# Strided attention on one core: eighteen pair buffers instead of sixteen quad buffers, one eviction per group

## The chip, the cores and the metric

The kernel runs on one core of a Trainium2 chip. The metric is the device time of one execution in microseconds; the median over three runs is given with its lowest and highest. A profile of one execution shows what each engine and the DMA queue did. Its span runs from the first to the last instruction and is a little shorter than the device time.

## What is computed

Q, K and V are float32 arrays of shape (8, 12, 1024, 64): 96 heads, 1024 positions, 64 channels. With stride 64, each query attends to the 16 positions 0, 64, 128, ... of its head:

```python
attend_positions = np.arange(0, seq, stride)
k = K[:, :, attend_positions, :]
v = V[:, :, attend_positions, :]
scores = np.einsum('bhqd,bhkd->bhqk', q, k) / np.sqrt(dim)
weights = np.exp(scores - np.max(scores, axis=-1, keepdims=True))
weights = weights / (np.sum(weights, axis=-1, keepdims=True) + 1e-10)
result[:, :, i, :] = np.einsum('bhqk,bhkd->bhqd', weights, v)[:, :, 0, :]
```

All of Q is read (25.2 MB), the output has the same size, and of K and V only one row in 64 is read. There are 1,024 times 96 rows of 16 scores.

## The kernel before

**Groups.** The 96 heads are cut into 24 groups of four heads (`NG`, `HG`). A group is 1 MB of Q and 1 MB of output, 128 partitions of 2048 float32 each. A buffer `qn[g % BUFS]` first receives a group of Q and later holds the same group's output, from which it is stored. There are 16 such buffers, in four tiles (`quads`) of four groups, so that a store of four groups reads one contiguous run of each partition.

**One group's way through the engines.** GpSimd casts Q to bfloat16 (`cast`, line 306; the first three are shared with ScalarE). VectorE transposes it in 32 x 32 blocks (`transpose`, line 317). TensorE makes the scores against the group's 16 keys per head (`score_products`). VectorE takes each row's maximum and subtracts it (`largest`). ScalarE takes the exponential (`raise_`, line 347). VectorE sums and takes reciprocals (`sums`). GpSimd multiplies (`weights`, line 359). TensorE transposes the weights (`turn_products`), ScalarE spreads them into a block layout with two instructions (`spread`, line 378), TensorE multiplies with the values (`output_products`, eight products into four PSUM banks, `o_ps`), and ScalarE evicts the result into the group's buffer (`evict`, line 406). The eviction is in two halves of 1024 columns: half 0 after the first four products, half 1 after the other four. There is one `o_ps`, so the products of group g+1 wait for the evictions of group g, half by half.

**The order of the work.** `Program` records every operation in one list, with what it reads and writes, and derives from it the semaphore waits; each engine executes its operations in the order of the list. The list is written by the loop over `i` at line 507, which calls the steps of `ORDER` (line 506) for group `i` minus the number behind the step's name. So in step i, ScalarE spreads group i-3, evicts group i-4 and takes the exponential of group i-1.

**TensorE's loop and the gates.** TensorE's instructions are a hardware loop of 14 passes with two turns each (`pe_stream`, line 512), so 28 turns for 24 groups: turn i makes the scores of group i, turns the weights of group i-2 and multiplies out group i-3, each after waiting on a counting semaphore called a gate: `turned`, `weighted`, `free0`, `free1`. The first and last turns work on dummy groups; dummy operations (`free`, a no-op on ScalarE; memsets of `edge`; counts of three) raise the gates for them. An instruction that raises a gate raises no other semaphore, so whoever waits for such an instruction waits for the next one on the same engine that doesn't raise a gate (line 103).

**Loads and stores.** All go through SP and one DMA queue. First the strided rows of K, then group 0, the rows of V, and groups 1 to 15. Each transfer is issued with a hand-built instruction, `_copy` (line 25). `queue` (line 468) puts the stores into SP's order: `STORES` gives runs of 4, 2, 2, 4, 4, 4, 2 and 2 groups. After the third store SP issues the eight late loads (groups 16 to 23), each of which waits for the store that empties its buffer. The last store is issued outside the list (line 537), after ScalarE's last eviction; GpSimd meanwhile waits for the older stores and clears the semaphores.

Of the kernel before, what the change touches and what calls it, by code (L numbers as in the profile page):

```python
# [168 lines left out]
def kernel(  # L169
# [14 lines left out]
    P = 128  # L184
# [6 lines left out]
    BUFS = 16  # L191
    RUN = 4
# [6 lines left out]
    quads = [sb.tile([P, RUN, 32 * D], FP32, name=f"quad{i}") for i in range(BUFS // RUN)]  # L199
    qn = [quads[i // RUN][:, i % RUN] for i in range(BUFS)]  # L200
# [7 lines left out]
    k_t = sb.tile([P, NG + 4, 2, 4 * NK], BF16, name="k_t")  # L208
    v_all = sb.tile([P, NG + 4, 4, D], BF16, name="v_all")
# [101 lines left out]
    def transpose(g):  # L311
        k_in = {0: "0", 1: "1"}.get(g)
        words = qt[g % 2].bitcast(I32)
        if g >= NG:
            op("DVE", lambda: nc.vector.memset(edge[:, g - NG : g - NG + 1], 0.0), gate="turned", times=1 if g == NG else 3)
# [42 lines left out]
    def weights(g):  # L358
        op("POOL", lambda: nc.gpsimd.tensor_tensor(  # L359
            out=wt[g % 2], in0=ex[g % 2],  # L360
            in1=rec[g % 2].unsqueeze(2).to_broadcast([P, 32, NK]), op=ALU.mult,
        ), reads=[f"ex{g % 2}", f"rec{g % 2}"] + [k for k in apart if k[0] == "v"], writes=[f"wt{g % 2}"], gate="weighted", times=1 if g < NG - 1 else 3)
# [33 lines left out]
    def outputs(g, n):  # L396
        op("PE", None, reads=[f"wb{g % 2}0", f"wb{g % 2}1"] + [
               f"v{g % 2}{a}{b}{int(g >= 4)}" if 0 <= g < NG else "none" for a in range(2) for b in range(2)
           ], writes=[f"o{n}"], gates=[(f"free{n}", g + 1)] if g >= 0 else [], looped=True)

    def evict(g, n):
        to = qn[g % BUFS].rearrange("p (b c x d) -> p c b (x d)", b=2, c=4, d=D)
        half = slice(2 * n, 2 * n + 2)
        plain = g >= NG - 1 - 2 * n
        ready = [f"wb{(g + 1) % 2}0", f"wb{(g + 1) % 2}1"] * (n == 0)
        op("ACT", lambda: nc.scalar.copy(  # L406
            to[:, half], o_ps[:, half].rearrange("p c (b x) -> p c b x", b=2)
        ), reads=[f"o{n}"] + ready, writes=[f"qn{g % BUFS}{n}"],
           gate=None if plain else f"free{n}", last=g == NG - 1 and n == 1)

        if plain:
            free([f"qn{g % BUFS}{n}"], n)

    def free(reads, n):
        op("ACT", lambda: nc.scalar.nop(), reads=reads, gate=f"free{n}")  # L415

    def send(g, n):
# [3 lines left out]
            _ap_with(qn[g % BUFS], [quads[0].ap[0], [1, 1], [1, 32 * n * D]]),  # L421
# [6 lines left out]
    def idle(i):  # L428
        scores(i)
        turn(i - 2)  # L430
        for n in range(2):
            outputs(i - 3, n)
# [29 lines left out]
    turns = (NG + 4) // TURN  # L462

    STORES = [4, 2, 2, 4, 4, 4, 2, 2]
    assert sum(STORES) == NG
    STORED = {sum(STORES[: i + 1]) - 1: n for i, n in enumerate(STORES)}

    def queue(g):
        if g not in STORED or g == NG - 1:
            return  # L470
        store(g - STORED[g] + 1, STORED[g])
        if g == NG - BUFS - 1:
            for n in range(BUFS, NG):
                load(n)

    def at(i, stage, lag):
# [5 lines left out]
        elif stage == "scores" and 0 <= g < NG + 4:  # L482
# [3 lines left out]
        elif stage == "turn" and 0 <= g < NG + 2:  # L486
            turn(g)
        elif stage in ("outA", "outB") and -1 <= g < NG + 1:
            outputs(g, int(stage == "outB"))
        elif stage == "spread" and 0 <= g < NG:  # L490
            spread(g)
        elif stage in ("evA", "evB") and g == -1:
            n = int(stage == "evB")
            free(["wb00", "wb01"], n)
        elif stage in ("evA", "evB") and 0 <= g < NG:
            evict(g, int(stage == "evB"))
# [9 lines left out]
    ORDER = "transpose0 cast-1 turn3 spread3 sums2 values2 weights2 outA4 largest1 evA4 outB4 evB4 scores0 raise_1 queue4".split()  # L506
# [5 lines left out]
    def pe_stream(sems, gates):  # L512
# [3 lines left out]
        for n in range(2):  # L516
            pe.sem_inc(gates[f"free{n}"], 3)
        with pe.Fori(0, turns) as turn_:
            for j in range(TURN):
# [5 lines left out]
                for n in range(2):  # L525
# [11 lines left out]
    end = send(NG - STORES[-1], STORES[-1])  # L537
# [34 lines left out]
```

## Time and profile before

| | |
|---|---|
| Median of 3 runs | 128.75 us (128.72 to 128.87) |
| The profiled execution: its own time | 128.75 us |
| The profiled execution: span | 126.9 us |
| TensorE matmuls, busy | 66.9 us (53%) |
| VectorE, busy | 88.0 us (69%) |
| ScalarE, busy | 97.6 us (77%) |
| GpSimd, busy | 75.9 us (60%) |
| Moved by DMA | 51.16 MB, 403 GB/s over the span |
| Granted TensorE clock, mean | 0.86 |

Times in the profile are in microseconds from the start of the span. PE is TensorE, PEld its weight loads, DVE VectorE, ACT ScalarE, POOL GpSimd, SP SyncE; SPq is SP's own instruction queue. A line of the slices gives, for 40 equal slices of the span, the busy share in tenths (9 means 90% or more). A row of a DMA queue gives packets, MB, and the time that its packets took as a share of 16 engines' span. A row of the stretches gives from:to and length, then for each engine the busy time with the number of instructions, then the granted TensorE clock, the DMA engines' busy share and the GB/s. A row of the timeline gives start, duration, engine, line and operation, with written tile, read tile and count, and in brackets the idle time before it and what ended it. A row of the DMA view gives the size and the time from issue to landing. A row of the waits gives who waited for whom: microseconds in total, times, longest. A row for one line's instructions gives durations in ns: least, median, greatest.

### The profile page before, as it was taken

Reading aid. Unit: us, or ns where it says so; the run is one execution under the profiler, and the core shown is the slowest. Engines: PE = TensorE matmul, PEld = TensorE weight load, DVE = VectorE, ACT = ScalarE, POOL = GpSimd, SP = SyncE. Lnnn points to the kernel's source line nnn. Section 1 sums busy time; section 2 is a strip of 40 time slices with the busy share of each in tenths; the row PEclk is TensorE's granted clock in tenths of the full one; section 3 lists DMA queues with packets and bytes.
Section 4 is the critical chain, followed back from the end, with each engine's and each line's share of the span. In section 5 each row is a group of like instructions: output and inputs, shape, how many; then the busy total and the mean of one; then the engine's idle time right before and its main releaser. Section 6 shows DMA issues by size and latency. Waiting matters only on the chain.

```text
span 126.9 us, 2253 instructions
## 1 busy us (share of the span) xinstructions
PE 66.9 (53%) x784; PEld 49.3 (39%) x784; DVE 88.0 (69%) x131; ACT 97.6 (77%) x133; POOL 75.9 (60%) x67
## 2 busy tenths in 40 slices
PE   0005796677836456586530394557856478771000
PEld 0004585455734334364320373335624356550000
DVE  3585979999899999999980779999999773000000
ACT  4147758999999999999993199999999999991000
POOL 5637698999999777797403996777793332000000
PEclk9999999965799999959996579998599955999755
DMA  0999999899998989989999999999999999999980
GB/s 23 418 320 465 392 454 465 372 475 392 444 475 361 465 361 485 454 351 423 418 470 434 413 454 392 465 434 403 454 385 457 423 423 444 392 398 434 429 382 21
DMA packets 5413, 51.16 MB, mean 403 GB/s; under 512 B 3616, under 2 KB 3616, under 8 KB 3616
## 3 DMA queue, kind: packets, MB, share of 16 engines
q1 hardware_dynamic: 5408, 51.12, 95.8%
q14 instruction: 5, 0.04, 0.1%
HBM read 25.95 MB, written 25.17 MB: 403 GB/s over the span
## 4 chain that ended last, share of the span: by engine, by line
DMA 30%; ACT 22%; POOL 21%; DVE 6%; issue 6%; PE 4%; SPq 1%; ACTq 0%; POOLq 0%
DMA out_dram<-quad 14%; ACT quad L406 13%; POOL qb L306 12%; DMA quad<-in_Q_dram 10%; ACT wb_all L378 7%; POOL wt_all L359 6%; DMA v_raw<-in_V_dram 6%; DVE qt L317 3%; ACT ex L347 3%; POOL v_all L288 2%; PE o L386 2%; DVE total L352 1%; SPq L34 1%; PE tp L366 1%; DVE top L339 1%
## 5 line engine op out<-in xcount | busy, mean ns | idle before, releaser
L406 ACT COPY quad<-o 128x1024 f32<-128x1024 f32 x48 | 46.3, 1015 | 2.2
L306 POOL CAST qb<-quad 128x2048 bf16<-128x2048 f32 x21 | 39.7, 1889 | 6.9 <-DMA quad<-in_Q_dram 6.8
L386 PE MATMUL o<-v_all,wb_all 128*128 x224 | 39.0, 317 | 2.4 <-ACTq L415 0.7
L359 POOL TENSOR_TENSOR wt_all<-ex,rec 128x512 bf16<-128x512 f32 x24 | 25.4, 1057 | 18.5 <-DVE rec L355 18.1
L378 ACT ACTIVATE wb_all<-tp,sel 128x512 bf16<-128x512 bf16 x48 | 30.4, 690 | 5.6 <-PE tp L366 5.4
L317 DVE STREAM_TRANSPOSE qt<-qb 128x1024 int32<-128x1024 int32 x24 | 29.7, 1237 | 5.2 <-POOL qb L306 5.0
L325 PE MATMUL sc<-k_t,qt 128*128 x448 | 23.3, 210 | 16.2 <-DVE qt L317 11.8
L325 PEld LDWEIGHTS sc<-k_t,qt 128*128 128x128 bf16 x448 | 20.4, 109 | 21.8 <-issue 19.6
L366 PE MATMUL tp<-identity,wt_all 128*128 128x128 bf16 x112 | 13.0, 249 | 29.8 <-POOL wt_all L359 29.8
L386 PEld LDWEIGHTS o<-v_all,wb_all 128*128 128x128 bf16 x224 | 22.9, 114 | 11.2 <-ACT quad L406 4.9
L352 DVE TENSOR_REDUCE total<-ex 128x32 f32<-128x512 f32 x24 | 16.3, 677 | 7.0 <-ACT ex L347 7.0
L366 PEld LDWEIGHTS tp<-identity,wt_all 128*128 128x128 bf16 x112 | 7.6, 109 | 32.6 <-POOL wt_all L359 32.6
L342 DVE TENSOR_TENSOR low<-sc,top 128x512 f32<-128x512 f32 x24 | 16.6, 691 | 0.8
L347 ACT ACTIVATE ex<-low 128x512 f32<-128x512 f32 x24 | 15.4, 641 | 2.1 <-DVE low L342 2.0
L339 DVE TENSOR_REDUCE top<-sc 128x32 f32<-128x512 f32 x24 | 15.2, 632 | 1.3 <-PE sc L325 1.3
L355 DVE RECIPROCAL rec<-total 128x32 f32<-128x32 f32 x24 | 8.5, 353 | 0.8
L288 POOL CAST v_all<-v_raw 32x128 bf16<-32x128 f32 (+1 forms) x12 | 5.2, 430 | 1.1 <-DMA v_raw<-in_V_dram 0.4
L302 POOL CAST qb<-quad 128x1024 bf16<-128x1024 f32 x3 | 3.1, 1037 | 4.3 <-DMA quad<-in_Q_dram 4.2
L300 ACT CAST qb<-quad 128x1024 bf16<-128x1024 f32 x3 | 3.1, 1045 | 2.4 <-DMA quad<-in_Q_dram 2.4
L264 ACT CAST k_half<-k_raw 128x768 bf16<-128x768 f32 x1 | 0.8, 831 | 3.2 <-DMA k_raw<-in_K_dram 3.2
L260 POOL MEMSET v_all<- 128x3584 f32 x1 | 3.1, 3085 | 0.0
L288 ACT CAST v_all<-v_raw 32x640 bf16<-32x640 f32 x4 | 2.9, 722 | 0.0
(15 smaller groups left out, 10.3 us busy)
## 6 DMA issues: line engine op xcount, KB each, us to landing
quad<-in_Q_dram SPq DMA_DIRECT2D x24, 1024.0 KB, 17.3
out_dram<-quad SPq DMA_DIRECT2D x4, 4096.0 KB, 18.3
out_dram<-quad SPq DMA_DIRECT2D x4, 2048.0 KB, 12.8
k_raw<-in_K_dram SPq DMA_DIRECT2D x1, 384.0 KB, 4.9
v_raw<-in_V_dram SPq DMA_DIRECT2D x1, 384.0 KB, 7.0
```

Of the source, the lines that this page charges most:

```text
L306: op("POOL", lambda: nc.gpsimd.tensor_copy(out=b, in_=q), reads=[f"qn{g % BUFS}{h}" for h in range(2)] + apart, writes=[f"qb{g % 2}{h}" fo ...
L317: op("DVE", lambda: nc.vector.transpose(_ap_with(words, [words.ap[0], [1, 2], [D, 16], [2, 32]]), qb[g % 2].bitcast(I32),), reads=[f"qb{g ...
L325: r = nc.tensor.matmul(sc_ps[g % 2][:, 64 * i : 64 * i + 64], lhsT=_ap_with(qt[g % 2], [qt[g % 2].ap[0], [2, P]], extra_offset=2 * P * i + f),
L339: op("DVE", lambda: nc.vector.tensor_reduce(out=m, in_=s, op=ALU.max, axis=mybir.AxisListType.X,), reads=[f"sc{g % 2}"], writes=[f"top{g % ...
L342: op("DVE", lambda: nc.vector.tensor_tensor(out=low, in0=s, in1=m.unsqueeze(2).to_broadcast([P, 32, NK]), op=ALU.subtract,), reads=[f"sc{g ...
L347: op("ACT", lambda: nc.scalar.activation(out=ex[g % 2], in_=low, func=AF.Exp, bias=0.0, scale=scale,), reads=["low"], writes=[f"ex{g % 2}"])
L352: op("DVE", lambda: nc.vector.tensor_reduce(out=total[g % 2], in_=ex[g % 2], op=ALU.add, axis=mybir.AxisListType.X,), reads=[f"ex{g % 2}"] ...
L359: op("POOL", lambda: nc.gpsimd.tensor_tensor(out=wt[g % 2], in0=ex[g % 2], in1=rec[g % 2].unsqueeze(2).to_broadcast([P, 32, NK]), op=ALU.mult,
L366: r = nc.tensor.transpose(tp_ps[g % 2][:, 2 * c : 2 * c + 2].rearrange("p a b -> p (a b)"), wt[g % 2][:, 8 * c : 8 * c + 8].rearrange("p t ...
L378: op("ACT", lambda a=a: nc.scalar.activation(out=wb[g % 2][:, :, 64 * a : 64 * a + 64], in_=tp_ps[g % 2], func=AF.Copy, scale=sel[:, a : a ...
L386: r = nc.tensor.matmul(_ap_with(o_ps, [o_ps.ap[0], [128, 2], [256, 2], [1, D]], extra_offset=512 * c + D * u,), lhsT=wb[g % 2][:, 2 * c + ...
L406: op("ACT", lambda: nc.scalar.copy(to[:, half], o_ps[:, half].rearrange("p c (b x) -> p c b x", b=2)), reads=[f"o{n}"] + ready, writes=[f" ...
```

## The change

- The buffers become 18, in nine tiles (`pairs`) of two groups. Eighteen loads stand in front; six are late.
- Stores are of two groups, in order, the last two groups in a store each. After the store of groups 2-3 SP gets the loads of 18 and 19, after 4-5 those of 20 and 21, after 6-7 those of 22 and 23. A load waits for the landing of the store that empties its buffer, as before. The step `queue` moves from lag 4 to lag 5.
- A group's output is evicted by one ScalarE instruction of 2048 columns, and one gate, `free`, stands for all of `o_ps`. Eight products follow one wait.
- TensorE's loop has 13 passes of two turns, 26 turns; the output products of the last group are recorded behind the loop with ordinary waits. The dummies for the last turns go, as do the no-ops on ScalarE; the second half of group 0's spread raises the gate for the dummy group -1. `k_t` and `v_all` have fewer slots.
- The rows of K and V are loaded with the library's `dma_start` instead of the hand-built copy.

```diff
-    BUFS = 16
-    RUN = 4
+    BUFS = 18
+    RUN = 2
...
-        op("SP", lambda: _copy(
-            nc, tile_, _ap_with(src, kv_src),
-        ), writes=[name], lane=lane)
+        op("SP", lambda: nc.sync.dma_start(tile_, _ap_with(src, kv_src)),
+           writes=[name], lane=lane)
...
-            ), reads=[f"tp{g % 2}", "sel"], writes=[f"wb{g % 2}{a}"])
-
-    def output_products(g, k, n):
-        for c in range(2 * n, 2 * n + 2):
+            ), reads=[f"tp{g % 2}", "sel"], writes=[f"wb{g % 2}{a}"], gate="free" if a and not g else None)
+
+    def output_products(g, k):
+        for c in range(4):
...
+    def outputs(g):
+        last = g == NG - 1
+        op("PE", (lambda: output_products(g, g + 3)) if last else None, reads=[f"wb{g % 2}0", f"wb{g % 2}1"] + [
                f"v{g % 2}{a}{b}{int(g >= 4)}" if 0 <= g < NG else "none" for a in range(2) for b in range(2)
-           ], writes=[f"o{n}"], gates=[(f"free{n}", g + 1)] if g >= 0 else [], looped=True)
+           ], writes=["o"], gates=[("free", g + 1)] if g >= 0 and not last else [], looped=not last)
...
         op("ACT", lambda: nc.scalar.copy(
-            to[:, half], o_ps[:, half].rearrange("p c (b x) -> p c b x", b=2)
-        ), reads=[f"o{n}"] + ready, writes=[f"qn{g % BUFS}{n}"],
-           gate=None if plain else f"free{n}", last=g == NG - 1 and n == 1)
+            to, o_ps.rearrange("p c (b x) -> p c b x", b=2)
+        ), reads=["o"], writes=[f"qn{g % BUFS}{n}" for n in range(2)], gate="free" if g < NG - 2 else None,
+           last=g == NG - 1)
...
-    turns = (NG + 4) // TURN
-
-    STORES = [4, 2, 2, 4, 4, 4, 2, 2]
+    turns = (NG + 2) // TURN
...
     def queue(g):
-        if g not in STORED or g == NG - 1:
-            return
-        store(g - STORED[g] + 1, STORED[g])
-        if g == NG - BUFS - 1:
-            for n in range(BUFS, NG):
-                load(n)
+        if g == NG - 2:
+            store(g, 1)
+        elif g % RUN == RUN - 1 and g < NG - 1:
+            store(g - RUN + 1, RUN)
+            late = BUFS + g - 2 * RUN + 1
+            if BUFS <= late < NG:
+                for n in range(late, late + RUN):
+                    load(n)
...
-    ORDER = "transpose0 cast-1 turn3 spread3 sums2 values2 weights2 outA4 largest1 evA4 outB4 evB4 scores0 raise_1 queue4".split()
+    ORDER = "transpose0 cast-1 turn3 spread3 sums2 values2 weights2 out4 largest1 evict4 scores0 raise_1 queue5".split()
...
-                for n in range(2):
-                    pe.wait_ge(gates[f"free{n}"], j + 1)
-                    output_products(j + 1, i, n).then_inc(done, 1)
-            for name in ("turned", "weighted", "free0", "free1"):
+                pe.wait_ge(gates["free"], j + 1)
+                output_products(j + 1, i).then_inc(done, 1)
+            for name in ("turned", "weighted", "free"):
                 pe.sem_inc(gates[name], -TURN)
...
-    end = send(NG - STORES[-1], STORES[-1])
+    end = send(NG - 1, 1)
```

More of the change, by code (lines that the diff above doesn't have):

```diff
@@ L198 @@
     edge = sb.tile([P, 32], FP32, name="edge")
-    quads = [sb.tile([P, RUN, 32 * D], FP32, name=f"quad{i}") for i in range(BUFS // RUN)]
-    qn = [quads[i // RUN][:, i % RUN] for i in range(BUFS)]
+    pairs = [sb.tile([P, RUN, 32 * D], FP32, name=f"pair{i}") for i in range(BUFS // RUN)]
+    qn = [pairs[i // RUN][:, i % RUN] for i in range(BUFS)]
     k_raw = sb.tile([P, NC, D], FP32, name="k_raw")
@@ L361, in weights @@
             in1=rec[g % 2].unsqueeze(2).to_broadcast([P, 32, NK]), op=ALU.mult,
[L362 removed]
+        ), reads=[f"ex{g % 2}", f"rec{g % 2}"] + [k for k in apart if k[0] == "v"], writes=[f"wt{g % 2}"], gate="weighted")
     def turn_products(g):
@@ L481, in at @@
             transpose(g)
-        elif stage == "scores" and 0 <= g < NG + 4:
+        elif stage == "scores" and 0 <= g < NG + 2:
             scores(g)
@@ L515, in pe_stream @@
         pe.sem_inc(gates["weighted"], 2)
-        for n in range(2):
-            pe.sem_inc(gates[f"free{n}"], 3)
+        pe.sem_inc(gates["free"], 3)
         with pe.Fori(0, turns) as turn_:
```

37 lines of the change are left out of this document (11 added, 26 removed).

## The prediction

> **What bounds the kernel now.** I read the page's slices first, then the queues, then stretches of the span.
>
> ```profile
> span 126.9 us, 2253 instructions
> ...
> DMA  0999999899998989989999999999999999999980
> ...
> q1 hardware_dynamic: 5408, 51.12, 95.8%
> ```
>
> ```profile
> 0.00:2.60 2.60, 0.00 (x0) 0.00 (x0) 0.67 (x1) 1.28 (x1) 1.20 (x7) 1.00 0.05 13
> ...
> 85.00:115.00 30.00, 20.73 (x235) 14.87 (x236) 17.97 (x30) 28.61 (x38) 12.66 (x10) 0.83 0.99 422
> 115.00:123.00 8.00, 0.28 (x3) 0.00 (x0) 0.00 (x0) 0.00 (x0) 0.00 (x0) 0.73 1.01 430
> ```
>
> The last two numbers of a stretch are the DMA engines' busy share and GB/s. The 16 engines are idle for 2.6 us, then full to about 123 us, 8 us longer than any compute engine works. Every load and store goes through one queue, in the order in which SP issues it. So the bound is that queue's 51 MB, and the question for each edit is whether it shortens the queue's work or opens a hole in it.
>
> What a transfer costs in a full queue is the distance between landings. A landing is the issue's start (SP's timeline, first number) plus the time to landing (last number of the transfer's row in the DMA view of that moment). Below are the second and the last of the first 16 loads, the eight stores, and the last of the eight late loads:
>
> ```profile
> 3.28 2.31 SPq L34 DMA_DIRECT2D quad<-in_Q_dram  x1
> 14.51 0.59 SPq L34 DMA_DIRECT2D quad<-in_Q_dram  x1
> 38.13 0.61 SPq L34 DMA_DIRECT2D out_dram<-quad  x1
> 45.52 0.58 SPq L34 DMA_DIRECT2D out_dram<-quad  x1
> 52.91 0.54 SPq L34 DMA_DIRECT2D out_dram<-quad  x1
> 66.81 0.60 SPq L34 DMA_DIRECT2D quad<-in_Q_dram  x1
> 67.70 0.59 SPq L34 DMA_DIRECT2D out_dram<-quad  x1
> 87.30 0.59 SPq L34 DMA_DIRECT2D out_dram<-quad  x1
> 102.08 0.54 SPq L34 DMA_DIRECT2D out_dram<-quad  x1
> 108.95 0.54 SPq L34 DMA_DIRECT2D out_dram<-quad  x1
> 115.78 0.54 SPq L34 DMA_DIRECT2D out_dram<-quad  x1
> ```
>
> ```profile
> quad<-in_Q_dram SPq DMA_DIRECT2D x1, 1024.0 KB, 8.8
> quad<-in_Q_dram SPq DMA_DIRECT2D x1, 1024.0 KB, 31.6
> out_dram<-quad SPq DMA_DIRECT2D x1, 4096.0 KB, 17.9
> out_dram<-quad SPq DMA_DIRECT2D x1, 2048.0 KB, 15.5
> out_dram<-quad SPq DMA_DIRECT2D x1, 2048.0 KB, 13.4
> quad<-in_Q_dram SPq DMA_DIRECT2D x1, 1024.0 KB, 18.8
> out_dram<-quad SPq DMA_DIRECT2D x1, 4096.0 KB, 28.2
> out_dram<-quad SPq DMA_DIRECT2D x1, 4096.0 KB, 18.8
> out_dram<-quad SPq DMA_DIRECT2D x1, 4096.0 KB, 14.3
> out_dram<-quad SPq DMA_DIRECT2D x1, 2048.0 KB, 12.3
> out_dram<-quad SPq DMA_DIRECT2D x1, 2048.0 KB, 10.4
> ```
>
> The landings, line by line: 12.1, 46.1, 56.0, 61.0, 66.3, 85.6, 95.9, 106.1, 116.4, 121.2, 126.2. The distances: 34.0 for 14 loads (2.43 each); 9.9 for the first 4 MB store; 5.0 and 5.3 for two of 2 MB, the second with loads right behind it; 19.3 for eight loads (2.41 each); 10.3, 10.2, 10.3 for three of 4 MB; 4.9 and 4.9 for two of 2 MB. They add up to 80.1 us from 46.1 to 126.2, and the span ends 0.7 later. The last store is issued at 115.78 while the one ahead of it lands at 121.2: compute is already 5.4 us ahead of the queue at the end.
>
> Compute has one large hole, in the middle:
>
> ```profile
> POOL qb L306 <- DMA quad<-in_Q_dram: 6.8, 2, 6.2
> ```
>
> The 17th load goes into the first store's buffer and is issued when that has landed (56.0); GpSimd's cast waits 6.2 us for it. In those microseconds the DMA engines are full all the same.
>
> **The buffers and the order on SP.** The sum is made against the profiled execution: 128.75 us with 126.9 of span, so 1.85 lie around the span; the median of the runs is 128.75 too. 18 loads now stand in front, so the last of them lands two loads later: 46.1 + 2 x 2.4 = 50.9. Stores of two groups follow as groups are evicted; SP's order is store 0-1, store 2-3, loads 18-19, store 4-5, loads 20-21, store 6-7, loads 22-23, then stores alone. Loads 18-19 wait for the landing of store 0-1 (50.9 + 5.0 = 55.9), and store 4-5 is queued on SP behind them though its groups are ready earlier. Does the queue run empty meanwhile? At 55.9 it still holds store 2-3, 5 us of work. Loads 20-21 are issued when that lands (about 61) with loads 18-19 and store 4-5 ahead of them, about 10 us; loads 22-23 likewise (about 71). So no hole. Loads 18-19 land at about 66. Group 16 was wanted at 62.5 (68.76, the start of the late cast, less 6.24 of wait), so at 3.7 us a group, below, group 18 is wanted at 69.9: the 6.2 us wait goes. What is late next is nothing that the end sees: compute only gets further ahead of the queue. I cost the removed wait at nothing.
>
> ```profile
> 68.76 1.89 POOL L306 CAST qb<-quad 128x2048 bf16<-128x2048 f32 x1 [6.24 <-DMA quad<-in_Q_dram]
> ```
>
> **The stores' size.** The bytes stay: 24 MB out, in eleven stores of 2 MB and two of 1 MB instead of eight stores. Price of 2 MB: 4.9 where the compute engines have finished, 5.0 while they work, half of 10.2 to 10.3 (5.1 to 5.15) inside a large store, 5.3 with loads right behind. The last is partly paid back: 5.3 + 19.3 = 24.6, against 5.0 + 8 x 2.43 = 24.4 (2.43 from the first loads), so a store ahead of loads costs 0.15 more, net. The sum over the landings: two more loads in front 4.9; six later loads 14.6; store 0-1 5.0; three stores ahead of loads 3 x 5.15 = 15.5; five stores while compute works at 5.07 (between 5.0 and 5.13), 25.3; the one at which compute ends 5.0; then 2 MB and 2 x 1 MB at 4.9 each, 9.8. Together 80.1, and before also 80.1: **0.0**. With every store at 4.9 and no charge for the alternation it would be 58.8 + 19.5 = 78.3, 1.8 less; with 5.15 for seven and 5.3 net for three, 36.1 + 15.9 + 9.8 + 19.5 = 81.3, 1.2 more. For busy stores I take a middle because the one clean row of this size under load (5.0) and the halves of the large ones disagree by 0.1.
>
> The Trainium skill, "DMA: Bandwidth & Descriptors", section Anatomy of one DMA, speaks against this part: it fits a DMA's time as about 2.0 us fixed plus bytes at 436 GB/s, so 6.8 us for 2 MB, and five more stores would be 10 us more if none of it overlapped. The 4.9 us between landings of 2 MB stores shows that in a full queue it overlaps.
>
> The final store shrinks from 2 MB to 1 MB. It stands behind its predecessor in a queue that is still full, so its size moves nothing: 0, or 0.1 for smaller packets.
>
> **The K and V loads' issue form.** They are the one edit ahead of the full stretch.
>
> ```profile
> 0.95 0.73 SPq L34 DMA_DIRECT2D k_raw<-in_K_dram  x1
> 1.74 0.83 SPq L34 DMA_DIRECT2D quad<-in_Q_dram  x1
> 2.61 0.62 SPq L34 DMA_DIRECT2D v_raw<-in_V_dram  x1
> ```
>
> ```profile
> L34 SPq DMA_DIRECT2D quad<-in_Q_dram x24: 471/596/2307, 1.7 to 66.8; - x24
> ```
>
> The engines start at about 2.5 us because K's issue begins at 0.95; whatever K's issue gets shorter moves the whole full stretch forward. No row shows the new form. Bounds by the nearest rows: as short as the shortest issue, 0.47, for both, 0.26 + 0.15 = 0.4 less; as long as the 0.83 beside them, 0.1 + 0.2 = 0.3 more. I take **-0.05**, near nothing: same bytes in the same 256-byte rows.
>
> **TensorE's loop, the gate, the single eviction.** All of this is compute, ahead of the queue. Its cover:
>
> ```profile
> 84.81 1.93 ACT L406 COPY quad<-o 128x1024 f32<-128x1024 f32 x2
> 86.63 0.64 ACT L347 ACTIVATE ex<-low 128x512 f32<-128x512 f32 x1
> 88.51 1.93 ACT L406 COPY quad<-o 128x1024 f32<-128x1024 f32 x2
> 89.97 1.76 PE L386 MATMUL o<-v_all,wb_all 128*128 x8
> 97.20 1.30 PE L386 MATMUL o<-v_all,wb_all 128*128 x8
> ```
>
> ScalarE paces a group: 88.51 - 84.81 = 3.70 us. One copy of 2048 columns instead of two of 1024 costs between 1.93 (nothing saved) and 1.76 (a single copy's 1.01 plus twice the step from 0.64 at 512 to 1.01 at 1024). The Trainium skill, "ScalarE: Activation LUTs", section What ACT_TABLE_LOAD costs, gives 186 ns plus 0.833 per element, by which it would be 1.89. Against it stands the one gate: TensorE may start a group's output products only when all of the previous group is evicted. Until ScalarE wants them it has 88.51 - 86.74 = 1.77 us; eight products take 1.30 us in one group above and 1.76 in another. Behind them on TensorE wait the next scores, for which VectorE's maximum waits. So the pitch goes to somewhere between 3.5 and 3.9. Without the 6.2 us hole the last store is issued near 115.78 - 6.2 = 109.6 at the old pitch. Its predecessor lands at about 126.2 - 2.5 = 123.7; I allow 2.5 us of lead and want the issue by 121. That is 11 us of cover for some 20 groups: under 4.2 us a group nothing shows. Cost **0**. The loop's missing turn and the dropped dummies end inside the same cover. So does one late signal: an eviction that raises the gate raises no other semaphore, so store 20-21 waits for ScalarE's next weights instruction and is queued one step later on SP, with store 22 and the last one behind it.
>
> Sum: 0.0 - 0.05, rounded: 126.85 of span, **128.7 us**.
>
> **Rivals.**
> *Small stores drain cleanly.* The three late large stores land 10.2 to 10.3 apart, two small ones 9.8. If the extra 0.4 belongs to the large form, every 2 MB store costs 4.9 to 5.0. For: the 5.0 row under load. Against: the 4.9 rows lie where compute has ended, so the load may be the reason. At 4.9 with 3 x 0.15 for alternation, 58.8 + 0.45 + 19.5 = 78.75: 127.35; at 5.0 for ten, 128.3. Middle 127.8.
> *Slower: alternation of direction.* Stores ahead of loads go from one to three, the places where loads turn to stores from two to four. The 5.3 row is all that shows a turn; if two more such turns, with what follows them, cost 0.35 each and are not caught up, +0.7: 129.4. It decides above 0.13 a turn, where two pass 0.2%. Against it: eight loads behind the one turn land 2.41 apart, which is catching up.
> *The queue runs dry.* A load held on SP by a late landing, or a pitch above 4.2. At 5 us of cover the first is far; 4.4 a group would cost 20 x 0.2 = 4 us: 132.7.
> *Each store pays its start alone.* K's 0.38 MB takes 4.9 us from issue to landing, 3.9 more than its bytes at 2.5 us a MB; five more stores exposed so give about 148.
>
> ```profile
> k_raw<-in_K_dram SPq DMA_DIRECT2D x1, 384.0 KB, 4.9
> ```
>
> The Trainium skill's fixed 2.0 (the page and section named above) would give 138.7 for that case.
> *The buffers don't remove the wait.* If a load still came late, compute would lag by the old 6.2 and the queue would still be full: the forecast again.
>
> **How the numbers follow.** About 0.2% (0.26 us) is what a measurement of this kernel can tell from no change. Forecast, 128.4 to 129.0: 0.54. Clean small stores: 0.22. Alternation: 0.17. Dry queue 0.05, exposed starts 0.02. Faster by over 0.2%: 0.22 and 0.14 of the forecast's lower edge, 0.36. Slower: 0.17 + 0.07 and 0.01 of its upper edge, 0.25. Within: 0.39. The range takes in most of the clean case and the alternation's middle: 127.7 to 129.4; outside lie about 0.06 below and 0.14 above.
>
> **What would show it.** GpSimd's 6.2 us row gone; the last store issued before 113; DMA digits full from slice 1 to 38; first 18 loads landed near 51; stores of 2 MB 4.9 to 5.2 apart. Clean stores: 4.9 apart while compute works. Alternation: over 5.3 at the stores ahead of loads. A slice of DMA under 8 in the middle would refute the whole reasoning; a first packet more than 0.3 us earlier or later, the front's term.

## The result, and the profile after

The changed kernel takes 128.0 us (median of 7 runs, 127.63 to 128.38); the kernel before took 128.75 beside it (7 runs, 128.66 to 128.87). The ratio is 0.9944, with a 95% interval of 0.9929 to 0.996: 0.75 us faster. The forecast was 128.7, in a range from 127.7 to 129.4. The profiled execution of after is its fastest run, 127.63 us, with 125.8 of span and 1.8 around it, so it lies 0.4 below the median; where a few tenths matter, medians are used.

The page of after, its span, its DMA slices and its queue:

```profile
span 125.8 us, 2084 instructions
...
DMA  1998989989899998999999999999999999999991
...
q1 hardware_dynamic: 6128, 51.12, 96.8%
```

There are 169 instructions fewer, the same 51.12 MB through one queue, and no slice under 8 in the middle. Before, the first slice had a 0; now it has a 1. That is the first place to read. The windows of after (the last two numbers are the DMA engines' share and GB/s):

```profile
0.00:2.60 2.60, 0.00 (x0) 0.00 (x0) 0.70 (x1) 1.28 (x1) 1.17 (x7) 1.00 0.08 20
...
85.00:106.00 21.00, 11.48 (x132) 8.03 (x132) 10.53 (x19) 18.97 (x21) 6.76 (x6) 0.92 1.00 425
106.00:115.00 9.00, 0.00 (x0) 0.00 (x0) 0.00 (x0) 0.70 (x1) 0.00 (x0) 0.50 1.02 431
```

The engines move more in the first 2.6 us (20 GB/s in place of 13). The compute engines are through at 106.7, 8 us sooner than before, and the queue goes on at the rate that it had. SP's timeline of after, the first three issues and two late stores:

```profile
0.96 0.43 SPq L236 DMA_DIRECT2D k_raw<-in_K_dram  x1
1.45 0.74 SPq L34 DMA_DIRECT2D pair<-in_Q_dram  x1
2.24 0.82 SPq L236 DMA_DIRECT2D v_raw<-in_V_dram  x1
...
86.55 0.54 SPq L34 DMA_DIRECT2D out_dram<-pair  x1
107.28 0.54 SPq L34 DMA_DIRECT2D out_dram<-pair  x1
```

and, from the DMA views of those moments, K's and V's loads and the same two stores (size, time to landing):

```profile
k_raw<-in_K_dram SPq DMA_DIRECT2D x1, 384.0 KB, 3.9
v_raw<-in_V_dram SPq DMA_DIRECT2D x1, 384.0 KB, 6.8
out_dram<-pair SPq DMA_DIRECT2D x1, 2048.0 KB, 23.8
out_dram<-pair SPq DMA_DIRECT2D x1, 1024.0 KB, 17.8
```

K's issue takes 0.43 us in place of 0.73. In all profiles where K comes first it is 0.43 to 0.44 in the library's form (nine) and 0.73 in the hand-built one (three). V's issue shows no such thing: it lasts 0.82 us here and 0.62 before, but 0.57 to 1.22 in the other profiles of the library's form and 0.62 to 1.03 in those of the hand-built one. From its issue K takes 3.9 us to land, where it took 4.9, but that scatters too (in the experiments 4.1 to 4.5 in this form and 4.4 to 4.5 in the other). What goes with the form of K's issue is the first packet of the queue. These are the GB/s of after, in 40 slices of the first 4 us, and of before, in 40 slices of the first 5 us:

```profile
GB/s 0 0 0 0 0 0 0 0 0 0 0 0 0 0 0 0 0 0 0 82 5 113 154 46 56 61 69 59 128 172 225 256 269 264 251 276 282 256 261 266
...
GB/s 0 0 0 0 0 0 0 0 0 0 0 0 0 0 0 131 66 0 0 18 88 70 61 68 47 127 215 250 258 270 244 197 195 209 182 700 1401 348 625 1131
```

The 82 of the first row and part of the slice behind the 5, and the 131 and 66 of the second, are fetches of instructions. K's first packet is in the slice with the 5, 2.0 to 2.1 us, and in that with the 18, 2.38 to 2.50 us. The packets themselves start at 2.08 and 2.46 us; over all profiles the nine have 2.07 to 2.09 and the three 2.46.

The last store is issued at 107.28 (before 115.78) and lands at 125.1. The last of the 18 first loads lands at 50.4. From there the distances between landings, from the trace's own times, which are finer than the rows, are 5.0 and 5.3 (stores), 4.7 (two loads), 5.0 (store), 4.8 (two loads), 5.2 (store), 4.7 (two loads), then the stores of 2 MB 5.3, 5.0, 5.1, 5.0, 4.9, 4.9 and 4.9, and the two of 1 MB 2.5 each. The one quoted from this tail lands at 86.55 + 23.8 = 110.3.

The groups of the page of after that answer to ScalarE's evictions and GpSimd's late casts (busy time, mean ns of one, idle time before them), and then, from the waits, TensorE's for the gate (in total, times, longest):

```profile
L403 ACT COPY pair<-o 128x2048 f32<-128x2048 f32 x24 | 47.9, 1995 | 2.8 <-PE o L385 2.8
L305 POOL CAST qb<-pair 128x2048 bf16<-128x2048 f32 x21 | 39.7, 1892 | 1.5 <-DMA pair<-in_Q_dram 1.5
```

```profile
PE o L385 <- ACT pair L403: 8.2, 18, 2.0
```

ScalarE's timeline of after, evictions of two neighbouring groups with the exponential behind the first, and the last eviction:

```profile
80.41 2.14 ACT L403 COPY pair<-o 128x2048 f32<-128x2048 f32 x1
82.16 0.93 ACT L346 ACTIVATE ex<-low 128x512 f32<-128x512 f32 x1
...
83.83 2.17 ACT L403 COPY pair<-o 128x2048 f32<-128x2048 f32 x1
...
104.83 1.87 ACT L403 COPY pair<-o 128x2048 f32<-128x2048 f32 x1 [1.98 <-PE o L385]
```

A group takes ScalarE 83.83 - 80.41 = 3.42 us, 0.28 less than before. One copy of 2048 columns takes 1.87 us by itself. In steady work its rows grow to 2.17 us, but they overlap those of the next instruction: from its start to that of the exponential it is 82.16 - 80.41 = 1.75 us, where the two copies of before had 86.63 - 84.81 = 1.82 us. Through the gate TensorE waits 8.2 us in all and at most 2.0 in one group; ScalarE waits 2.8 us for the products, 1.98 of it before the last eviction. GpSimd's casts wait 1.5 us for loads in all, where one wait took 6.2.

### The profile page after: what moved, and what is told of

Its sections match the earlier page's. It is cut to its first block, busy times and chain, and to the rows that moved or that the text cites. A ratio compares the mean times of both kernels' runs of the same rounds, so it can differ in the third digit from the quotient of the medians.

```text
span 125.8 us, 2084 instructions
## 1 busy us (share of the span) xinstructions
PE 58.1 (46%) x736; PEld 43.5 (35%) x736; DVE 87.1 (69%) x131; ACT 93.8 (75%) x109; POOL 75.9 (60%) x67
## 3 DMA queue, kind: packets, MB, share of 16 engines
q1 hardware_dynamic: 6128, 51.12, 96.8%
## 4 chain that ended last, share of the span: by engine, by line
ACT 51%; POOL 15%; DVE 7%; DMA 5%; PE 4%; issue 1%; SPq 1%; POOLq 0%
ACT pair L403 28%; ACT wb_all L377 16%; ACT ex L346 7%; POOL qb L305 6%; DMA v_raw<-in_V_dram 5%; POOL wt_all L358 4%; PE o L385 4%; POOL v_all L287 4%; DVE qt L316 3%; DVE total L351 1%; DVE top L338 1%; DVE rec L354 1%; POOL qb L301 1%; SPq L34 1%; DVE low L341 1%
## 5 line engine op out<-in xcount | busy, mean ns | idle before, releaser
L403 ACT COPY pair<-o 128x2048 f32<-128x2048 f32 x24 | 47.9, 1995 | 2.8 <-PE o L385 2.8
L305 POOL CAST qb<-pair 128x2048 bf16<-128x2048 f32 x21 | 39.7, 1892 | 1.5 <-DMA pair<-in_Q_dram 1.5
L385 PE MATMUL o<-v_all,wb_all 128*128 (+1 forms) x216 | 31.6, 295 | 8.2 <-ACT pair L403 8.2
L377 ACT ACTIVATE wb_all<-tp,sel 128x512 bf16<-128x512 bf16 x48 | 33.3, 810 | 0.7 <-PE tp L365 0.6
L324 PE MATMUL sc<-k_t,qt 128*128 x416 | 19.4, 200 | 12.9 <-DVE qt L316 12.8
L324 PEld LDWEIGHTS sc<-k_t,qt 128*128 128x128 bf16 x416 | 16.9, 103 | 17.5 <-issue 16.6
L346 ACT ACTIVATE ex<-low 128x512 f32<-128x512 f32 x24 | 18.3, 764 | 2.5 <-DVE low L341 2.5
L299 ACT CAST qb<-pair 128x1024 bf16<-128x1024 f32 x3 | 3.1, 1045 | 3.1 <-DMA pair<-in_Q_dram 3.1
L301 POOL CAST qb<-pair 128x1024 bf16<-128x1024 f32 x3 | 3.1, 1039 | 3.3 <-DMA pair<-in_Q_dram 3.3
L259 POOL MEMSET v_all<- 128x3456 f32 x1 | 3.0, 2979 | 0.0
```

Source lines behind the costliest of these rows:

```text
L305: op("POOL", lambda: nc.gpsimd.tensor_copy(out=b, in_=q), reads=[f"qn{g % BUFS}{h}" for h in range(2)] + apart, writes=[f"qb{g % 2}{h}" fo ...
L324: r = nc.tensor.matmul(sc_ps[g % 2][:, 64 * i : 64 * i + 64], lhsT=_ap_with(qt[g % 2], [qt[g % 2].ap[0], [2, P]], extra_offset=2 * P * i + f),
L346: op("ACT", lambda: nc.scalar.activation(out=ex[g % 2], in_=low, func=AF.Exp, bias=0.0, scale=scale,), reads=["low"], writes=[f"ex{g % 2}"])
L377: op("ACT", lambda a=a: nc.scalar.activation(out=wb[g % 2][:, :, 64 * a : 64 * a + 64], in_=tp_ps[g % 2], func=AF.Copy, scale=sel[:, a : a ...
L385: r = nc.tensor.matmul(_ap_with(o_ps, [o_ps.ap[0], [128, 2], [256, 2], [1, D]], extra_offset=512 * c + D * u,), lhsT=wb[g % 2][:, 2 * c + ...
L403: op("ACT", lambda: nc.scalar.copy(to, o_ps.rearrange("p c (b x) -> p c b x", b=2)), reads=["o"], writes=[f"qn{g % BUFS}{n}" for n in rang ...
```

## The experiments

Two explanations stood against each other. The **front theory**: the queue is full to the end, so the gain is what K's shorter issue moves the start forward, and everything else is worth nothing. The **body theory**: the smaller stores, the single eviction with its smaller code, or the earlier end of compute let the queue move its 51 MB faster. Ratios are to the kernel before, run on the same chip in the same job; its median there was 128.66, 128.68 and 128.69 us in the three jobs.

### The front alone, the rest alone, the stores alone

The kernel before with K and V issued in the library's form:

```diff
-        op("SP", lambda: _copy(
-            nc, tile_, _ap_with(src, kv_src),
-        ), writes=[name], lane=lane)
+        op("SP", lambda: nc.sync.dma_start(tile_, _ap_with(src, kv_src)),
+           writes=[name], lane=lane)
```

> The kernel before with one edit, the library's form of issue for the K and V rows. Front theory (the gain is the K and V issue: K's issue 0.44 instead of 0.73 us, the full stretch of the DMA queue about 0.7 us earlier): 128.05 us, the second load landing about 11.3 at the latest engine. Rival 'small stores' and rival 'buffers and compute': 128.75, no change, whatever the K issue takes.

It took 128.27 us, 0.39 less than before and 0.2 more than the front theory's figure: ratio 0.9969 (0.9955 to 0.9983). Its compute ends where that of before does (ScalarE at 114.2, the last store issued at 115.39), so these two lines alone give over half of the gain.

The changed kernel with the hand-built copy for K and V:

```diff
-        op("SP", lambda: nc.sync.dma_start(tile_, _ap_with(src, kv_src)),
-           writes=[name], lane=lane)
+        op("SP", lambda: _copy(
+            nc, tile_, _ap_with(src, kv_src),
+        ), writes=[name], lane=lane)
```

> The changed kernel with K and V issued by the hand-built copy again. Front theory: the gain is gone, 128.7 us, K's issue back at 0.73 us. Rivals 'small stores' or 'buffers and compute': 128.0, the gain stays.

It took 128.49 us, 0.17 less than before: 0.9983 (0.9975 to 0.9992). That lies between the two theories: all of the rest is worth 0.2, not nothing. Its K row on SP is that of before again:

```profile
0.95 0.73 SPq L34 DMA_DIRECT2D k_raw<-in_K_dram  x1
```

The kernel before with stores of two groups throughout:

```diff
-    STORES = [4, 2, 2, 4, 4, 4, 2, 2]
+    STORES = [2] * 12
```

> The kernel before with twelve stores of two groups and nothing else changed; late loads stay together behind the store of groups 6 and 7. Front theory: 128.75, within 0.2. Rival 'small stores': the large stores' 10.2 to 10.3 us become 2 x 4.9 to 5.0, so 128.05 or lower.

It took 128.84 us, 0.18 more than before: 1.0014 (1.0004 to 1.0025). Small stores are not what gives the 0.2; by themselves they cost about as much.

### Is it the length of the first issue, or K's form?

If only the length of the first issue counted, a Q load in front would start the queue as early, with big packets. The changed kernel with group 0 ahead of K:

```diff
-    load_rows("k_raw", k_raw, K, "k")
     load(0)
+    load_rows("k_raw", k_raw, K, "k")
+    load(1)
     load_rows("v_raw", v_raw, V, "v")
-    for g in range(1, BUFS):
+    for g in range(2, BUFS):
         load(g)
```

> The changed kernel with the order of the first transfers changed: group 0, K, group 1, V, group 2 and on, so that large packets fill the DMA engines while the 256-byte rows of K and V are being described. Front theory: whatever fills the queue sooner moves the end; 127.4 to 127.7 us, though compute starts some 1 us later. Rivals: 128.0, since neither stores nor buffers change, or slower if the later start of compute mattered (128.5 and more).

It took 128.30 us, 0.36 less than before (0.997; 0.9958 to 0.9982) and about 0.3 more than the changed kernel. The expectation failed. SP's first rows:

```profile
0.95 0.58 SPq L34 DMA_DIRECT2D pair<-in_Q_dram  x1
1.60 0.56 SPq L236 DMA_DIRECT2D k_raw<-in_K_dram  x1
```

The first issue here lasts 0.58 us, a hand-built one, against 0.43 for K in the library's form; the first packets of 32 KB start at 2.32 us where K's small ones start at 2.08. The GB/s of this kernel in 40 slices of the first 4 us show how they start (a packet counts in the slice in which it begins; the 164 and the 82 are fetches of instructions):

```profile
GB/s 0 0 0 0 0 0 0 0 0 0 0 0 0 0 0 0 0 0 0 164 0 82 0 2294 0 0 328 0 0 0 0 2294 328 0 0 0 0 0 0 0
```

Eight packets begin at 2.3 to 2.7 us and eight more only at 3.1 to 3.2 us. The first eight take 1.8 to 2.3 us each, the later ones 1.2 to 1.4. So this load in front didn't fill the engines sooner. The length of the first issue fits the order of the times: 0.43, 0.58 and 0.73 us go with first packets at 2.08, 2.32 and 2.46 us, and with 128.04 (the changed kernel, in the run below), 128.30 and 128.49 us. It isn't isolated here, because K also comes later and the last store is issued at 110.2 in place of 107.9. A Q load in front in the library's form wasn't run.

The changed kernel with the library's form for K only:

```diff
-        op("SP", lambda: nc.sync.dma_start(tile_, _ap_with(src, kv_src)),
-           writes=[name], lane=lane)
+        op("SP", lambda: (nc.sync.dma_start if lane == "k" else lambda o, i: _copy(nc, o, i))(
+            tile_, _ap_with(src, kv_src)), writes=[name], lane=lane)
```

> The changed kernel with only K issued in the library's form and V by the hand-built copy. If the first issue alone sets the start of the full stretch: 128.0, within 0.1 of the changed kernel. If both issues count alike: 128.2 to 128.3.

It took 127.99 us: 0.9946 (0.9931 to 0.996), all of the change's gain. K's issue is the term; V's, behind a load that is already in the queue, moves nothing that shows.

K and V issued from ScalarE's queue, so that SP begins with Q at once:

```diff
-        op("SP", lambda: nc.sync.dma_start(tile_, _ap_with(src, kv_src)),
+        op("ACT", lambda: nc.scalar.dma_start(tile_, _ap_with(src, kv_src)),
            writes=[name], lane=lane)
```

> The changed kernel with K and V issued from ScalarE's queue, so that SP issues group 0 at once, at 0.95 us. Front theory in its wide form (any earlier filling of the queue moves the end): 127.5 to 127.8. In its narrow form (what counts is when K's rows have been described and moved, whoever else moves beside them): 128.0.

It took 157.33 us: 1.2223 (1.22 to 1.2246), 29 us slower, the largest miss of the study. The page of this kernel, its DMA slices and its two queues:

```profile
DMA  4999999999997000000919989999999999997994
...
q1 hardware_dynamic: 3024, 50.33, 77.4%
q10 hardware_dynamic: 3104, 0.79, 2.2%
```

and the two loads in its DMA view, and ScalarE's timeline:

```profile
k_raw<-in_K_dram ACTq DMA_DIRECT2D x1, 384.0 KB, 48.2
v_raw<-in_V_dram ACTq DMA_DIRECT2D x1, 384.0 KB, 47.2
```

```profile
1.33 2.27 ACTq L236 DMA_DIRECT2D k_raw<-in_K_dram  x1
3.65 27.26 ACTq L236 DMA_DIRECT2D v_raw<-in_V_dram  x1
...
49.56 0.83 ACT L263 CAST k_half<-k_raw 128x768 bf16<-128x768 f32 x1 [17.34 <-DMA k_raw<-in_K_dram]
```

Q's first 18 loads run at full rate through slice 13, then the queue is empty for six slices, because no group can be computed without K, and K has only just come. The second queue holds 3104 packets, nearly all of 256 bytes, 194 to an engine, beside 18 MB in packets of 32 KB, 36 to an engine, and a closing packet of 4 bytes for each load, 18 to an engine. If an engine takes a packet from each queue in turn, only some 54 of its 194 small ones pass while the loads last, and the rest when they are through. That is what the trace shows: between 10 and 40 us it has 576 packets of the one queue and 576 of the other, between 8 and 48 us 840 of the second queue's 3104 (52 to an engine), and between 48 and 51 us 2261. So 0.38 MB takes 48.2 us, as long as the 18 loads. The Trainium skill, "DMA: Bandwidth & Descriptors", section Queues, rings and completion order, says that each DMA engine takes its queues in turn, packet by packet; the 576 against 576 agree with it. V's issue held ScalarE's queue for 27.26 us as well.

### Where the other 0.2 us is from

The changed kernel once more, beside the next three:

> The changed kernel once more, beside the next three on the same chip, as their measure. 128.0 to 128.1 us. If the two halves found so far (0.4 for the K and V issue, 0.2 for all the rest) add up, it is 0.6 below the kernel before.

It took 128.04 us: 0.9945 (0.993 to 0.996). The result stands on a second chip.

The eviction in two instructions, of which the second raises the one gate:

```diff
-        op("ACT", lambda: nc.scalar.copy(
-            to, o_ps.rearrange("p c (b x) -> p c b x", b=2)
-        ), reads=["o"], writes=[f"qn{g % BUFS}{n}" for n in range(2)], gate="free" if g < NG - 2 else None,
-           last=g == NG - 1)
+        for n in range(2):
+            half = slice(2 * n, 2 * n + 2)
+            op("ACT", lambda half=half: nc.scalar.copy(
+                to[:, half], o_ps[:, half].rearrange("p c (b x) -> p c b x", b=2)
+            ), reads=["o"], writes=[f"qn{g % BUFS}{n}"], gate="free" if n and g < NG - 2 else None,
+               last=n == 1 and g == NG - 1)
```

> The changed kernel with the eviction as two ScalarE instructions of 1024 columns again, the second raising the one gate. Cover theory (compute is far ahead of the queue): same as the changed kernel within 0.1 us. Fetch theory (the rest of the gain is one 8 KB instruction fetch less on the last DMA engine, since ScalarE has 24 instructions fewer): 0.2 to 0.3 slower, with a second late instruction fetch back in the trace.

It took 127.99 us: 0.9951 (0.9935 to 0.9967). It has 24 ScalarE instructions more, and after 80 us two fetches of instructions on the DMA engines, as the kernel before has, where the changed kernel has one. Neither shows in the time: the form of the eviction and the length of the code don't give the 0.2, as far as the intervals of some 0.2 us on either side can tell.

Sixteen buffers in place of eighteen:

```diff
-    BUFS = 18
+    BUFS = 16
```

> The changed kernel with 16 buffers: eight late loads in four pairs, one more turn of direction in the queue. Cover theory: within 0.15 us of the changed kernel, by the one turn slower if at all (0.13). 'Buffers and compute': 0.2 or more slower, the part of the gain that the K and V issue leaves.

It took 128.15 us: 0.9961 (0.9949 to 0.9973), 0.1 more than beside it, with intervals that overlap. Its waits:

```profile
POOL qb L305 <- DMA pair<-in_Q_dram: 9.3, 4, 4.8
```

GpSimd's wait for late loads is back, 9.3 us in all, and the last store is issued at 113.6 in place of 107.9. The removed wait is worth some 0.1, which these runs don't tell from nothing, nor from 0.3.

An extra copy on ScalarE ahead of each eviction, of 384 columns, that nobody reads, so that a group takes ScalarE about as long as before:

```diff
+    spare = sb.tile([P, 2, 768], BF16, name="spare")
...
         op("ACT", lambda: nc.scalar.copy(
+            spare[:, g % 2, 0:384], k_bf.rearrange("p n d -> p (n d)")[:, 0:384]
+        ), reads=["k_bf"], writes=[f"spare{g % 2}"])
+        op("ACT", lambda: nc.scalar.copy(
             to, o_ps.rearrange("p c (b x) -> p c b x", b=2)
```

> The changed kernel with one more ScalarE copy (384 columns, of no use) per group ahead of the eviction, about 0.4 us a group: the last store should be issued near 115 us, as in the kernel before, instead of 107. Cover theory: unchanged within 0.1 us. Drift theory (the last DMA engine falls behind the others only while the compute engines work): 0.2 to 0.4 slower, the last engine's landing further behind the median one.

It took 128.26 us: 0.998 (0.9963 to 0.9997), with a wide scatter (127.88 to 129.28). The last store is issued at 115.0 in place of 107.9, some 0.35 us a group later over 20 groups, and by the medians 0.2 us of the gain is given back: the level of the first experiment, which has only K's and V's form. The ratios, 0.998 against 0.9945, make it 0.4; a few long runs weigh there.

The same copy with 768 columns (in place of `0:384`):

```diff
+            spare[:, g % 2, 0:768], k_bf.rearrange("p n d -> p (n d)")[:, 0:768]
```

> The changed kernel with an extra ScalarE copy of 768 columns per group: about 4.2 us a group, last store issued near 121 to 122 us. Drift theory (the queue runs a little slower while the compute engines work): 128.3 to 128.5, no jump. Cover theory: still 128.0, or 129 and more if 122 is past the point where the queue runs dry.

It took 128.83 us: 1.0009 (0.9997 to 1.0021), 0.8 more than the changed kernel. Two neighbouring evictions on its ScalarE timeline, and two of its windows:

```profile
86.59 2.11 ACT L407 COPY pair<-o 128x2048 f32<-128x2048 f32 x1
90.74 2.12 ACT L407 COPY pair<-o 128x2048 f32<-128x2048 f32 x1
```

```profile
112.00:115.00 3.00, 1.44 (x12) 0.93 (x12) 0.00 (x0) 3.00 (x4) 0.32 (x1) 1.00 0.49 208
115.00:118.00 3.00, 0.57 (x3) 0.43 (x4) 0.00 (x0) 3.00 (x3) 0.00 (x0) 0.52 0.88 377
```

At 90.74 - 86.59 = 4.15 us a group compute is caught up by the queue at 112 us, and the rate falls to half: 208 GB/s where after had 425. The last store is issued at 121.8. Here the cover is gone, and only here.

The other side, less compute. From group 2 on this kernel leaves out the sums and reciprocals and the second half of the spread:

```diff
     def sums(g):
+        if g >= 2:
+            return
...
-        for a in range(2):
+        for a in range(2 if g < 2 else 1):
```

> The changed kernel with less computed: the sums and reciprocals of all groups but the first two are left out, and so is the second half of the spread, so that ScalarE and VectorE have about 0.7 and 1.0 us less a group and the last store is issued well before 107 us (as far as the loads allow). Its output is not the reference's. Drift theory: 0.1 to 0.2 faster than the changed kernel. Cover theory: 128.0.

It took 127.98 us: 0.9957 (0.994 to 0.9974). It doesn't tell the theories apart, because compute didn't end sooner. Evictions on its ScalarE timeline, early and late:

```profile
69.47 1.87 ACT L405 COPY pair<-o 128x2048 f32<-128x2048 f32 x1
72.55 1.87 ACT L405 COPY pair<-o 128x2048 f32<-128x2048 f32 x1
...
92.39 1.87 ACT L405 COPY pair<-o 128x2048 f32<-128x2048 f32 x1 [0.95 <-PE o L387]
96.32 1.87 ACT L405 COPY pair<-o 128x2048 f32<-128x2048 f32 x1 [0.95 <-PE o L387]
```

The pitch is 3.08 us until the groups of the last late loads are reached, which have to wait for them. After that it is 3.93: the granted clock is 0.59 from 88 to 108 us (0.88 in the changed kernel from 92 to 106), and with one gate TensorE's products and ScalarE's copy follow each other, so that ScalarE waits 0.95 us a group. The last store is issued at 109.6, later than in the changed kernel.

Side by side, the kernels by form of K's issue and by the time of the last store's issue:

| kernel | K's issue | last store issued | median us |
|---|---|---|---|
| changed, again | library | 107.9 | 128.04 |
| two evictions | library | 108.0 | 127.99 |
| K only | library | 107.9 | 127.99 |
| less compute | library | 109.6 | 127.98 |
| group 0 ahead of K | library, as the second | 110.2 | 128.30 |
| 16 buffers | library | 113.6 | 128.15 |
| before with K and V in the library's form | library | 115.4 | 128.27 |
| extra copy of 384 | library | 115.0 | 128.26 |
| extra copy of 768, queue dry at 112 | library | 121.8 | 128.83 |
| changed with the hand-built copy | hand-built | 108.9 | 128.49 |
| before | hand-built | 115.8 | 128.66 to 128.69 |
| before, small stores | hand-built | 115.8 | 128.84 |

Two steps can be read: 0.4 to 0.45 between the forms at the same end of compute, and 0.2 between an early and a late end in the same form. None of the variants is faster than the changed kernel by more than their scatter.

The kept traces show where in the queue the 0.2 lies. Take the landings apart at the last late load. Behind it every kernel of the table but the one with 16 buffers has the same 16 MB left to store, and between the 16th load and it they have moved the same bytes too. In after the last late load is this; by its rows it lands at 85.0 us, and at 85.1 in the trace's finer times, from which the table is worked out:

```profile
70.94 0.59 SPq L34 DMA_DIRECT2D pair<-in_Q_dram  x1
...
pair<-in_Q_dram SPq DMA_DIRECT2D x1, 1024.0 KB, 14.1
```

| profiles | last store issued | 16th load to last late load, us | last late load to last store, us |
|---|---|---|---|
| before; with K and V in the library's form; with small stores | 115.4 to 115.8 | 39.5, 39.7, 39.9 | 40.5, 40.5, 40.7 |
| after; again; hand-built copy; two evictions; K only; less compute | 107.3 to 109.6 | 39.6, 40.5, 40.2, 39.9, 40.0, 39.9 | 40.0, 39.9, 40.0, 40.0, 39.9, 39.9 |
| group 0 ahead of K | 110.2 | 40.0 | 40.1 |
| extra copy of 384 | 115.0 | 39.7 | 39.9 |
| extra copy of 768, queue dry at 112 | 121.8 | 40.1 | 40.4 |

The gain lies in the tail, half a microsecond, and the part ahead of it, in which the turns of direction lie, takes some of it back. In the tail of the kernel with small stores the stores of 2 MB land 5.1 to 5.2 apart while compute works and 4.9 apart at the end; in after they come down to 4.9 earlier. But the extra copy of 384 doesn't fit: with compute as late as before its tail is as short as after's. That profile is the fastest execution of its twelve (127.88 us). So a short tail goes with an early end of compute in all these profiles but one, which doesn't show it to be the cause.

## Why the prediction was right, and where it was not

The time lies inside the range, but 0.7 us under the forecast and below the forecast's own case (128.4 to 129.0): "no change" was held likelier than "faster" by a little, and it became faster. Two terms make some 0.6 of the 0.7, the form of K's issue and a 0.2 that the sum didn't have; the rest is no more than the medians scatter.

**The bound.** The queue full from end to end was right, and so, but for 0.2 us, was that compute's time doesn't count. Moving the last store's issue from 107.9 to 115.0 cost 0.2 us by the medians, and more only when the queue ran dry.

**The removed wait, at nothing.** Right as far as can be told: with 16 buffers 9.3 us of waiting come back, for 0.1 us that is within the scatter. The row of 6.2 us is gone in after.

**The stores' size, 0.0.** Priced rightly, but for the tail: in after 2 MB take 5.0 to 5.1 where compute works (5.3 for the store behind the last loads), 4.9 where it has ended, 5.0 to 5.3 ahead of loads. From the landing of the 16th load to that of the last store the profile of after has 79.6 us and the second one of the same kernel 80.4, against the 80.1 of the forecast, which is too coarse for the last 0.2. The parts are steadier. The sum's terms give 4.9 + 5.0 + 15.5 + 14.6 = 40.0 us up to the last late load, where the six profiles of the changed order have 39.6 to 40.5, and 25.3 + 5.0 + 9.8 = 40.1 us behind it, where they have 39.9 to 40.0. So the six stores taken at 5.07 and 5.0 us were taken too dear, by some 0.2 us in all.

**The K and V loads' issue form, -0.05.** This is the step that failed, in its size: "I take -0.05, near nothing: same bytes in the same 256-byte rows". The lower bound of the same step, 0.4 less, was the right answer: 0.39 less in the kernel before with only this edit, and 0.45 more when the changed kernel loses it. The reason was wrong too. K's bytes and rows didn't change, and yet its issue went from 0.73 to 0.43 us with the form of the instruction; what in the form makes it shorter wasn't looked into. That the bound came out is in part luck: its working split the gain over K (0.26) and V (0.15), and K alone gives all of it. K's issue is 0.30 shorter, and the first packet starts 0.38 sooner in the trace (2.08 in place of 2.46). The prediction named a first packet more than 0.3 us earlier as the sign that the front's term was wrong; that sign is there.

**TensorE's loop, the gate, the single eviction, at 0.** Right to 0.2 us. The pitch of 3.4 lies just under the 3.5 to 3.9 that were given; the one copy, at 1.75 from start to start, lies at the lower end of its 1.76 to 1.93; and the last store was issued at 107.3, ahead of the 109.6. The cover was taken a little too long: under 4.2 us a group nothing was to show, but at 4.15, with the last store at 121.8, the queue had run dry at 112 already and 0.8 us was lost. What was missing besides is the 0.2 us that goes with an earlier end of compute.

**The rivals.** Small stores that drain cleanly: refuted by the kernel before with small stores, 0.18 slower instead of 0.4 to 1.4 faster. Alternation of direction: in after the three stores ahead of loads land 5.3, 5.0 and 5.2 after what precedes them, the pairs of loads behind them 4.7 to 4.8, and from the 18th load to the last late one it is 34.7 us, against 34.6 for four stores at 5.0 and six loads at 2.43: what a turn costs is nearly paid back. In five other profiles of the same order that stretch has 35.0 to 35.6 us, so 0.14 to 0.35 a turn stays. The 0.15 of the sum fits; the total of 129.4 that this rival gave does not. The dry queue exists, but a group has to be slowed by 0.7 us to reach it. Starts that are paid alone show nowhere: 2 MB stores land 4.9 us apart here too. The fit of the Trainium skill that the prediction sets against that part ("DMA: Bandwidth & Descriptors", section Anatomy of one DMA) is stated there for DMAs that GpSimd issues; these go through SP. Buffers that don't remove the wait: nothing of it.

**What stays open.** Some 0.2 us of the gain goes with compute that ends 7 us sooner. The extra copy gave it back by the medians, in the only run that changes nothing else, and 16 buffers half of it. But that copy is itself more work beside the queue, its runs scatter, its own profile has the short tail, and one profile's last landing varies by as much. What connects the end of compute with a queue that is full either way wasn't found; the kernel that was to show it from the other side ended no sooner and so says nothing.

## What to carry to other kernels

Where the DMA slices are full from one end to the other, look at what comes before the first packet: here the first issue's own length was paid in full, and the same transfer issued in another form was worth more than new buffers, a removed wait of 6 us and 169 fewer instructions together. When a wait is off the bound, cost it at nothing, but work out at what pitch its cover ends. Be wary of putting a transfer of small rows that everything waits for on a second queue beside large ones; here it cost 29 us.

## What the runs showed of the hardware

- The two queues shared the engines by packets, not by bytes: 576 packets of each passed between 10 and 40 us, and 0.38 MB in 256-byte packets took 48.2 us beside packets of 32 KB, and 3.9 in front of them.
- A first load with large packets didn't start the flow sooner: 2.32 us to the first packet, against 2.08 for K's small ones, and half of its first 16 packets began only at 3.1 us. Its issue was a hand-built one of 0.58 us, against 0.43.
- In the last 2 us of the span few of the DMA engines still work: the mean busy share falls to 0.30, as if five of the 16 worked. Windows of after:

```profile
122.00:123.00 1.00, 0.00 (x0) 0.00 (x0) 0.00 (x0) 0.00 (x0) 0.00 (x0) 0.50 0.90 377
123.00:124.00 1.00, 0.00 (x0) 0.00 (x0) 0.00 (x0) 0.00 (x0) 0.00 (x0) 0.50 0.30 123
124.00:125.00 1.00, 0.00 (x0) 0.00 (x0) 0.00 (x0) 0.00 (x0) 0.00 (x0) 0.50 0.02 8
```

and of the kernel with the copy of 768 columns, whose queue had run dry at 112:

```profile
124.00:125.00 1.00, 0.00 (x0) 0.00 (x0) 0.00 (x0) 0.00 (x0) 0.00 (x0) 0.50 1.05 442
125.00:126.00 1.00, 0.00 (x0) 0.00 (x0) 0.00 (x0) 0.00 (x0) 0.00 (x0) 0.50 0.32 131
```

In after the rate falls at 123 and the last store lands at 125.1; in the other it is full until 125 and the last store lands at 126.0, one microsecond later. By their rates its two windows from 112 to 118 lost 3 x (1 - 208/425) + 3 x (1 - 377/425) = 1.9 us, but the kernel lost only 0.8, and this profile's execution, its fastest, 0.5. That late engines caught up in the hole would explain it; no run tested it.
